# Forming the low parts of the filler weights by an accumulating DMA

## The chip, the cores and the metric

The kernel runs on one NeuronCore of a Trainium2 chip. A core has engines that work side by side, each through its own instructions in order: TensorE (PE in the profile, with its weight loads as PEld), VectorE (DVE), ScalarE (ACT), GpSimd (POOL) and SyncE (SP), which here issues most DMAs. The number that counts is the device time of one execution in microseconds. The kernel before takes 875.28 us (median of 3 runs, 873.97 to 875.67).

## The reference

One decoder block on 512 tokens of width 1024. After a modulated RMSNorm, one wide projection `w_in` feeds two token mixers, multi-head latent attention (MLA) and native sparse attention (NSA). Each mixer's output goes through its own output weights, and a sigmoid gate for each token and channel, also a product with `w_in`, weighs the two before they are added:

```
y_mla = mla_attention(...) @ w_o_mla
y_nsa = nsa_attention(...) @ w_o_nsa
merged = sigmoid(g_mla_merge) * y_mla + sigmoid(g_nsa_merge) * y_nsa
x = x + gt1 * (merged @ w_out)
x = x + gt2 * ((silu(h2 @ w_gate) * (h2 @ w_up)) @ w_down)
```

`g_mla_merge` and `g_nsa_merge` are the last 2048 columns of `h @ w_in`.

## The kernel before

**High and low parts.** The matmuls take operands of type fp32r, which holds fewer bits than float32. To keep the precision the kernel splits every operand into a high part (the value rounded to fp32r) and a low part (what the rounding took away, again as fp32r) and makes three products: high by high, high by low, low by high. For weights this is done by `wchunk`: it loads a chunk of up to 128 x 1024 floats into a tile `raw` (on SP's queue), ACT copies it into `whi` (`hi_of`, line 169), and another engine subtracts, `raw - whi`, into `wlo` (`lo_of`, line 172). The three tiles come from one pool, `wp`, with four buffers for each name, and all weights of the kernel share them. So at most four chunks are in preparation or use. A buffer of `raw` is free again when the low part has been formed, one of `whi` or `wlo` when the last matmul with it is done. In the first half of the kernel, SP loads the next chunk into a `raw` buffer as soon as it is free, whichever job asks for it; among them are strips of `ada_w` for the modulation vectors, which DVE multiplies and adds up into `macc`.

**Stages.** The projection runs first, then NSA (about 160 to 300 us), then MLA's latent products (300 to 350), MLA's attention (350 to 440), the output projections and the feed-forward part. Almost every instruction is recorded by the helper at line 152, so the profile gives L152 for all of them, and its groups are told apart by their tiles.

**Fillers.** The attention stages have chains of small steps through PE, DVE and ACT: scores, row minimum and mask (`mn`, on DVE), exponential (`s`, on ACT), row sums and scaling (`sm`), transposition on PE (`pt`), a split into `phi` (ACT) and `plo` (DVE), and the product with the values (`av`). To keep PE busy meanwhile, two side jobs are woven in:

- `gates()` makes the products for the merge gates. It has 16 jobs of one weight chunk (128 columns over the full depth of 1024) and 24 matmuls `gp` each. At a job's end ACT evacuates the sum through a tanh into `gs` and stores it to DRAM (`spill`).
- `y_nsa()` makes `nsa output @ w_o_nsa`: four chunks, each used for two sums `yn`, which DVE multiplies by the stored gate and POOL's queue stores.

Eleven of the gate jobs belong to the NSA stage (`D_GATES = 88` steps of 8 for each job), one lies between the stages, four and all of `y_nsa` belong to MLA's attention (`F_FILL = 64` steps). Both jobs get their chunks from `ahead`, which asks for a chunk one job before it is used, and with the arguments of `fill_lo`: which engine makes the low part, and into how many pieces the chunk is cut. Before the change that is POOL while the NSA stage is written down and DVE from line 1212 on (`fill_on[0] = dve`), with `FILL_CUT = 2`: the chunk's two halves are split one after the other. Twelve chunks get their low part on POOL, eight on DVE.

**Order of the work.** The kernel is written in a tile language. Each engine's order is not the order of the text: at the build a planner simulates a timeline with estimated durations (`schedule_with_timeline_sim=True`, line 1856) and lets each engine take what is ready, earlier text first. So a chunk asked for in the text one job ahead may be loaded and split as soon as buffers are free. `Paced` adds a few order constraints by hand: filler matmuls may not run ahead of the main work by more than a given count (`PACE_D`, `PACE_F`).

**POOL's other work** in these stages: scaling the selected probabilities in NSA and one row block of four in MLA (`s<-s,sm`), the low parts of the attention outputs (`onl`, `oml`), small square root steps, and the stores of `y_nsa`.

Of the kernel before, what the change touches and what calls it, by code (L numbers as in the profile page):

```python
# [15 lines left out]
ALU = mybir.AluOpType  # L16
# [17 lines left out]
FILL_CUT = 2  # L34
# [81 lines left out]
def hybrid_block(ctx, tc, a, out):  # L116
# [47 lines left out]
    pe, act, dve, pool, sp = (Paced(e) for e in (nc.tensor, nc.scalar, nc.vector, nc.gpsimd, nc.sync))  # L164

    def f32v(ap):
        return ap.bitcast(F32)

    def hi_of(dst, src, scale=1.0):
        act.activation(out=dst, in_=src, func=AF.Copy, scale=scale)  # L170

    def lo_of(dst, src, hi, eng=None):
        (eng or dve).tensor_tensor(out=dst, in0=src, in1=f32v(hi), op=ALU.subtract)
# [106 lines left out]
    def wload(src, parts, n):  # L280
        raw = wp.tile([P, 1024], F32, name="raw", tag="raw")
        rv = raw[:, : parts * n].rearrange("p (a n) -> p a n", a=parts)
        sp.dma_start(out=rv, in_=src)
        return raw

    def wchunk(src, parts, n, eng_lo=None, cut=1):
        raw = wload(src, parts, n)
        h = wp.tile([P, 1024], F32R, name="whi", tag="whi")
        l = wp.tile([P, 1024], F32R, name="wlo", tag="wlo")
        m = parts * n // cut  # L290
        for i in range(cut):
            c = slice(i * m, (i + 1) * m)
            hi_of(h[:, c], raw[:, c])
            lo_of(l[:, c], raw[:, c], h[:, c], eng_lo)
        return (h[:, : parts * n].rearrange("p (a n) -> p a n", a=parts),
                l[:, : parts * n].rearrange("p (a n) -> p a n", a=parts))

# [3 lines left out]
    fill_on = [pool]  # L301

    def fill_lo():
        return fill_on[0], FILL_CUT

    turn_at = [0]

# [65 lines left out]
    def gemm_tok(A, w, kt, c0, n, consume, tag="", eng_lo=None):  # L373
        ps = [mm.tile([P, S], F32, name=f"g{tag}{t}", tag="mm") for t in range(NT)]
        for k0 in range(0, kt, 2):
            parts = min(2, kt - k0)
            h, l = wchunk(rows(w, k0 * P, parts, c0, n), parts, n, eng_lo)
            for i in range(parts):
                k = k0 + i
                for t in range(NT):  # L380
                    ah, al = A(k, t)
                    pe.matmul(ps[t][:, :n], ah, h[:, i, :], start=(k == 0), stop=False)
                    pe.matmul(ps[t][:, :n], ah, l[:, i, :], start=False, stop=False)
                    pe.matmul(ps[t][:, :n], al, h[:, i, :], start=False, stop=(k == kt - 1))
            yield
        for t in range(NT):
            consume(t, ps[t][:, :n])
            yield

    def gemm_wide(A, w, kt, c0, na, nb, consume_a, consume_b, pair_first=False, eng_lo=None):  # L390
        pa = [mm.tile([P, S], F32, name=f"wa{t}", tag="mm") for t in range(NT)]
        pb = [sc.tile([P, 2, 256], F32, name=f"wb{j}", tag="sc") for j in range(2)]
        n = na + nb
        sa, sb = (slice(nb, n), slice(0, nb)) if pair_first else (slice(0, na), slice(na, n))
        ready = []

        def fetch(k):
            ready.append(wchunk(rows(w, k * P, 1, c0, n), 1, n, eng_lo))

        fetch(0)  # L400
        for k in range(kt):
            h, l = ready.pop()
            for t in range(NT):
                if t == FETCH_AT and k + 1 < kt:
                    fetch(k + 1)
                ah, al = A(k, t)
                for o, cs in ((pa[t][:, :na], sa), (pb[t // 2][:, t % 2, :nb], sb)):
                    first = k == 0 and (cs is sa or t % 2 == 0)
                    pe.matmul(o, ah, h[:, 0, cs], start=first, stop=False, skip_group_check=True)
                    pe.matmul(o, ah, l[:, 0, cs], start=False, stop=False, skip_group_check=True)  # L410
                    pe.matmul(o, al, h[:, 0, cs], start=False, stop=(k == kt - 1), skip_group_check=True)
            yield
        for t in range(NT):
            consume_a(t, pa[t][:, :na])
            if t % 2 == 1:
                consume_b(t - 1, pb[t // 2][:, 0, :nb])
                consume_b(t, pb[t // 2][:, 1, :nb])
            yield
# [435 lines left out]
    def compress_w1(i, nm):  # L854
        FS = cmp_state[i]
        ph = sc.tile([P, S], F32, name="ph", tag="sc") if i else mm.tile([P, S], F32, name="ph", tag="mm")
        cmp_state[i] = ph
        w1 = a[f"cmp_w1_{nm}"][0]
        for k0 in range(0, 16, 4):
            h, l = wchunk(rows(w1, k0 * P, 4, 0, 256), 4, 256)  # L860
            for j in range(4):
                pe.matmul(ph[:, :256], FS[:, k0 + j, :], h[:, j, :], start=(k0 + j == 0), stop=False)
                pe.matmul(ph[:, :256], FS[:, k0 + j, :], l[:, j, :], start=False, stop=(k0 + j == 15))
            yield
# [220 lines left out]
    def gates():  # L1085
        jobs = [(rows(w_in, 0, KD, SEG_C + c, P), KD, P) for c in range(0, 2 * D, P)]
        for i, (h, l) in enumerate(ahead(jobs, FILL_LEAD, fill_lo)):
            ps = mm.tile([P, S], F32, name="gp", tag="mm")
            for k in range(KD):
                turned_mm([ps], 0, hT[k], h[:, k, :], l[:, k, :], k == 0, k == KD - 1)  # L1090
                if k == KD - 1:
                    spill(ps, i)
                yield

    def y_nsa():
        jobs = [(rows(a["w_o_nsa"][0], 0, 4, c, 256), 4, 256) for c in range(0, D, 256)]
        for i, (h, l) in enumerate(ahead(jobs, FILL_LEAD, fill_lo)):
            for j in range(2):
                ps = mm.tile([P, S], F32, name="yn", tag="mm")
                at = 2 * i + j  # L1100
                gate = spill_src["pool"].tile([P, S], F32, name="gx", tag="gx", bufs=1)
                sp.dma_start(out=gate, in_=spilled[2 + at // 4][at % 4])
                for k in range(4):
                    turned_mm([ps], j * P, (on_h[k], on_l[k]), h[:, k, :], l[:, k, :], k == 0, k == 3)
                    if k == 3:
                        spill(ps, 16 + at, gate)
                    yield
# [752 lines left out]
```

## Time and profile before

| | |
|---|---|
| median of 3 runs | 875.28 us |
| profiled execution | 874.82 us |
| its span, first to last instruction | 873.0 us |
| PE busy | 841.4 us (96%) |
| DVE busy | 668.7 us (77%) |
| ACT busy | 457.2 us (52%) |
| POOL busy | 119.2 us (14%) |
| DMA, all queues | 115.54 MB, 132 GB/s |

All times of the trace are microseconds from the first instruction. A row of a group reads: line, engine, operation, output tile `<-` input tiles, shape, count, then busy time, mean duration in ns, and the idle time of that engine just before, with what ended it. "POOL waits for ACT whi" means that the last thing that POOL needed was ACT's instruction that writes `whi`. An engine's idle time matters only where PE, or the end of the kernel, waits for that engine. The granted clock (PEclk) is the share of full speed at which TensorE may run. The profiled execution's 874.82 us contain the span of 873.0 us and 1.8 us around it.

### The profile page before, as it was taken

To read this page: it belongs to the slowest core of one execution; us is meant where nothing else is said; L and a number is where in the kernel's file an instruction comes from. 1 tells how busy PE (TensorE), PEld (TensorE's weight loads), DVE (VectorE), ACT (ScalarE), POOL (GpSimd) and SP (SyncE) were. 2 spreads that over 40 slices of the span, in tenths; PEclk is the share of its full clock that TensorE was granted. 3 is DMA by queue.
4 is the path that set the end of the run, shared out by engine and by line. 5 is a ranking of instruction groups with operands and counts; after the bars stand their busy time and mean duration, and the time that the engine had idled before them with its cause. 6 is when DMAs were issued, how large, how long until landed. Compare 5 with 4: busy or idle time off the path is not lost.

```text
span 873.0 us, 13961 instructions
## 1 busy us (share of the span) xinstructions
PE 841.4 (96%) x5052; PEld 740.4 (85%) x5052; DVE 668.7 (77%) x1392; ACT 457.2 (52%) x962; POOL 119.2 (14%) x203
## 2 busy tenths in 40 slices
PE   8899799899999999899999999999999999999997
PEld 8789689777777789787788889898999889988996
DVE  5778896668888568688879877975887858965875
ACT  4643655678666567665634255551456326641550
POOL 0002516525342012212200000000000000000000
PEclk9999799999999999999999999999999999999999
DMA  9956646222201123325597753452233313343312
GB/s 309 326 166 189 197 143 170 74 72 74 72 13 61 43 92 98 120 97 180 172 321 253 256 166 118 128 152 90 73 98 121 121 51 113 104 125 92 98 49 97
DMA packets 95706, 115.54 MB, mean 132 GB/s; under 512 B 6565, under 2 KB 68885, under 8 KB 95637
## 3 DMA queue, kind: packets, MB, share of 16 engines
q1 hardware_dynamic: 92596, 108.32, 40.4%
q10 hardware_dynamic: 2400, 4.23, 1.3%
q0 software_dynamic: 640, 2.10, 0.6%
q8 instruction: 40, 0.66, 0.3%
q14 instruction: 30, 0.24, 0.1%
HBM read 106.24 MB, written 8.39 MB: 131 GB/s over the span
## 4 chain that ended last, share of the span: by engine, by line
PE 79%; DVE 8%; DMA 7%; ACT 3%; issue 2%; SPq 1%; ACTq 0%; DVEq 0%
PE d L152 14%; PE fx L152 12%; PE gp L152 9%; PE fy L152 9%; PE pt L152 4%; DMA strip<-in_ada_w_dram 4%; PE av L152 3%; PE ga L152 3%; PE gwo L152 3%; PE gym L152 3%; PE fg L152 3%; PE yn L152 3%; PE wo L152 3%; PE gq L152 2%; PE fu L152 2%
## 5 line engine op out<-in xcount | busy, mean ns | idle before, releaser
L152 ACT ACTIVATE whi<-raw 128x1024 fp32r<-128x1024 f32 (+4 forms) x161 | 141.6, 897 | 133.1 <-PE d L152 51.6
L152 DVE TENSOR_TENSOR wlo<-raw,whi 128x1024 fp32r<-128x1024 f32 (+4 forms) x138 | 149.4, 1090 | 61.3 <-ACT whi L152 60.8
L152 PE MATMUL d<-whi,mh 128*128 128x512 f32 (+1 forms) x180 | 69.9, 391 | 0.6 <-DVE tm L152 0.5
L152 PE MATMUL d<-wlo,mh 128*128 128x512 f32 (+1 forms) x180 | 70.2, 390 | 0.0
L152 PE MATMUL d<-whi,ml 128*128 128x512 f32 (+1 forms) x180 | 67.6, 389 | 0.0
L152 ACT ACTIVATE s<-s,mn 128x384 f32<-128x384 f32 (+2 forms) x96 | 52.5, 548 | 23.1 <-DVE mn L152 22.5
L152 DVE TENSOR_TENSOR plo<-pt,phi 128x512 fp32r<-128x512 f32 (+2 forms) x78 | 46.3, 602 | 19.1 <-ACT phi L152 18.7
L152 PE MATMUL gp<-hTh,whi 128*128 128x512 f32 x128 | 54.4, 425 | 0.0
L152 ACT ACTIVATE phi<-pt 128x512 fp32r<-128x512 f32 (+2 forms) x78 | 39.9, 525 | 27.5 <-PE pt L152 26.9
L152 PE MATMUL gp<-hTh,wlo 128*128 128x512 f32 x128 | 51.2, 400 | 0.0
L152 PE MATMUL gp<-hTl,whi 128*128 128x512 f32 x128 | 50.7, 396 | 0.0
L152 ACT ACTIVATE whi<-s 128x1024 fp32r<-128x1024 f32 (+1 forms) x36 | 30.2, 846 | 32.0 <-PE d L152 18.0
L152 PEld LDWEIGHTS d<-whi,mh 128*128 128x128 f32 x180 | 33.7, 188 | 8.9 <-DVE tm L152 1.2
L152 PE MATMUL fx<-h2h,whi 128*128 128x256 f32 x144 | 41.1, 286 | 0.0
L152 PE MATMUL fx<-h2l,whi 128*128 128x256 f32 x144 | 40.8, 283 | 0.0
L152 PE MATMUL fx<-h2h,wlo 128*128 128x256 f32 x144 | 40.8, 283 | 0.0
L152 PEld LDWEIGHTS d<-whi,ml 128*128 128x128 f32 x180 | 33.8, 188 | 7.7
L152 PEld LDWEIGHTS d<-wlo,mh 128*128 128x128 f32 x180 | 33.8, 188 | 7.4
L152 DVE TENSOR_TENSOR wlo<-s,whi 128x1024 fp32r<-128x1024 f32 (+1 forms) x36 | 33.7, 951 | 7.4 <-ACT whi L152 7.4
L152 PE MATMUL pt<-ident,s 128*128 128x128 f32 x232 | 37.4, 278 | 0.1
L152 POOL TENSOR_TENSOR wlo<-raw,whi 128x512 fp32r<-128x512 f32 x24 | 31.7, 1341 | 23.1 <-ACT whi L152 23.1
L152 PEld LDWEIGHTS pt<-ident,s 128*128 128x128 f32 x232 | 28.1, 142 | 7.6 <-issue 2.1
(432 smaller groups left out, 2666.2 us busy)
## 6 DMA issues: line engine op xcount, KB each, us to landing
raw<-in_ffn_w_gate_dram SPq DMA_DIRECT2D x22, 512.0 KB, 3.9
raw<-in_ffn_w_up_dram SPq DMA_DIRECT2D x22, 512.0 KB, 4.1
raw<-in_ffn_w_down_dram SPq DMA_DIRECT2D x22, 512.0 KB, 3.9
raw<-in_ada_w_dram SPq DMA_DIRECT2D x18, 512.0 KB, 5.0
araw<-in_ada_w_dram SPq DMA_DIRECT2D x32, 256.0 KB, 6.4
raw<-in_w_in_dram SPq DMA_DIRECT2D x16, 512.0 KB, 4.8
strip<-in_ada_w_dram SPq DMA_DIRECT2D x14, 512.0 KB, 5.2
raw<-in_w_in_dram SPq DMA_DIRECT2D x12, 352.0 KB, 3.2
```

The costliest lines, as they stand in the source:

```text
L152: out = call(*args, **kw)
```

## The change

The filler chunks, and only they, get their low part in another way. ACT writes the negated high part into `wlo` (the same rounding of the same values, with a scale of -1), and then a DMA on POOL's queue adds `raw` to what stands in `wlo`. The sum `raw - whi` is the same as before. The chunk is no longer cut in two, and `fill_lo` says so for all 20 filler chunks, whatever `fill_on` holds.

```
         for i in range(cut):
             c = slice(i * m, (i + 1) * m)
             hi_of(h[:, c], raw[:, c])
-            lo_of(l[:, c], raw[:, c], h[:, c], eng_lo)
+            if eng_lo == "dma":
+                hi_of(l[:, c], raw[:, c], -1.0)
+                pool.dma_start(out=l[:, c], in_=raw[:, c], accum_op=ALU.add)
+            else:
+                lo_of(l[:, c], raw[:, c], h[:, c], eng_lo)
...
     def fill_lo():
-        return fill_on[0], FILL_CUT
+        return "dma", 1
```

All other weights keep their subtraction on DVE. The buffer of `raw` is now in use until the DMA has landed.

## The prediction

> **What bounds the kernel now.** I read the page first, then busy time by stretch, then the waits of PE in the stretch that the edit touches, then the chain of waits.
>
> ```profile
> span 873.0 us, 13961 instructions
> ...
> PE 841.4 (96%) x5052; PEld 740.4 (85%) x5052; DVE 668.7 (77%) x1392; ACT 457.2 (52%) x962; POOL 119.2 (14%) x203
> ```
>
> PE is busy for 841.4 of 873.0 us, so 31.6 us of the span are not matmul time. The edit touches the 20 weight chunks of the two fillers (16 of the merge gates, 4 of the NSA output), which are prepared and used between 145 and 447 us. This is the busy time by stretch there (columns: us, then PE, weight loads, DVE, ACT, POOL, with instructions in brackets, then clock, DMA share, GB/s).
>
> ```profile
> 165.00:300.00 135.00, 130.77 (x654) 102.18 (x655) 104.59 (x312) 93.48 (x261) 46.00 (x62) 0.97 0.18 55
> 300.00:348.00 48.00, 46.99 (x258) 42.77 (x257) 33.71 (x96) 33.05 (x115) 10.01 (x38) 1.00 0.30 86
> 348.00:447.00 99.00, 94.19 (x513) 78.02 (x511) 77.69 (x190) 59.04 (x150) 19.00 (x32) 1.00 0.49 159
> sum 302.00, PE 290.82 PEld 240.37 DVE 224.16 ACT 196.19 POOL 87.60; mean PE 72.71 PEld 60.09 DVE 56.04 ACT 49.05 POOL 21.90
> ```
>
> The sum row covers 145 to 447 us: PE stands still for 302.0 - 290.8 = 11.2 us in it, DVE is busy for 74%, ACT for 65%, POOL for 29%. Those 11.2 us are the most that any relief of another engine can win, clock aside, since the edit leaves every matmul as it is. Who is last when PE waits:
>
> ```profile
> PE ps L152 <- DVE mn L152: 4.0, 6, 1.8
> PE av L152 <- ACT phi L152: 2.6, 5, 1.6
> PE pw L152 <- DVE mn L152: 2.1, 4, 0.6
> PE gk L152 <- ACT whi L152: 0.6, 1, 0.6
> PE pw L152 <- DVE sm L152: 0.6, 1, 0.6
> PE gk L152 <- DVE wlo L152: 0.4, 1, 0.4
> PE av L152 <- DVE plo L152: 0.2, 1, 0.2
> ```
>
> (total us, times, longest.) These are softmax statistics (mn, sm) and turned probabilities (phi, plo), apart from 1.0 us at gk, whose chunks the edit leaves alone. No wait of PE for the low part of an edited chunk is here: gp and yn are not in the list.
>
> **The change, part by part.** The rows that price it:
>
> ```profile
> L152 POOL TENSOR_TENSOR wlo<-raw,whi 128x512 fp32r<-128x512 f32 x24 | 31.7, 1341 | 23.1 <-ACT whi L152 23.1
> L1076 POOL DMA_DIRECT2D spill<-gs x8 | 4.8, 601 | 31.7 <-DVE gs L152 15.5 <-DVE mn L152 9.8 <-DVE sm L152 6.4
> L152 DVE TENSOR_TENSOR wlo<-raw,whi 128x512 fp32r<-128x512 f32 x16 | 10.4, 684 | 1.4 <-ACT whi L152 1.3
> L152 ACT ACTIVATE whi<-raw 128x1024 fp32r<-128x1024 f32 x88 | 93.4, 1062 | 113.0 <-PE d L152 51.6 <-PE fy L152 18.1 <-DMA raw<-in_w_out_dram 9.0
> ...
> spill<-gs POOLq DMA_DIRECT2D x8, 256.0 KB, 3.9
> raw<-in_w_in_dram SPq DMA_DIRECT2D x16, 512.0 KB, 4.8
> ```
>
> *Removed.* The 24 POOL and 16 DVE subtractions on half chunks: 31.7 us of POOL, 10.4 us of DVE. 24 + 16 halves are the 20 chunks.
>
> *Added on ACT.* One negated copy for each chunk, of the same size as a whole high part: 20 x 1.062 = 21.2 us. The high part itself is made in one piece where it was two; two halves in a row occupy 1.15 us (rows below) against 1.06, so 20 x 0.09 = 1.8 us go. Net +19.4 us: ACT between 145 and 447 us goes from 196.2 to 215.6 of 302 us, 65% to 71%.
>
> *Added on POOL.* 20 DMA issues. The eight plain ones on this queue take 0.60 us each, so about 12 us; POOL is still 31.7 - 12 = 20 us lighter. Each issue waits for ACT's negated copy where the subtraction waited for the high part, 1.06 us earlier. Behind it in POOL's queue stand the scaling of the selected probabilities, the low parts of the attention outputs and, later, the stores of gated rows. POOL is busy for 19.0 of 99 us in the last stretch and in nobody's row among the waits of PE, so I take 0.
>
> *Added on the DMA engines.* 20 transfers of 512 KB that also read their destination. No row shows an accumulating transfer. Near end: 3.9 us to landing for a plain 256 KB one from this queue. Far end: three streams of 512 KB (read source, read destination, write) instead of two of 256 KB, three times that, 11.7 us. I take 6, a little above the 4.8 us of a plain 512 KB load, and keep both ends. Nothing below 3.9 is likely, as the plain transfer is half the size.
>
> *How late a low part may be.* Low part and PE's use of it lie far apart (the first row: duration min/median/max in ns, first and last start; the others: start, us, what):
>
> ```profile
> L152 PE MATMUL gp<-hTh,wlo x9: 392/397/628, 159.5 to 175.8; 128*128 128x512 f32 x9
> ...
> 146.52 1.15 ACT L152 ACTIVATE whi<-raw 128x512 fp32r<-128x512 f32 x2 [3.55 <-PE ga L152]
> ...
> 158.38 1.15 ACT L152 ACTIVATE whi<-raw 128x512 fp32r<-128x512 f32 x2
> 159.44 0.37 ACT L152 ACTIVATE KH<-pk 128x256 fp32r<-128x256 f32 x1
> ...
> 172.54 1.15 ACT L152 ACTIVATE whi<-raw 128x512 fp32r<-128x512 f32 x2 [0.20 <-POOL s L152]
> ...
> 209.28 0.58 ACT L152 ACTIVATE gs<-gp 128x512 f32<-128x512 f32 x1
> ```
>
> Four buffers of each kind let ACT take up the fifth chunk at 172.5 us; the fourth job is evacuated (gs) at 209.3, and only then is the fifth chunk needed: 37 us. The new path from the start of the high part is 1.06 + 1.06 + 0.60 + 6 = 8.7 us, at the far end 14.4. So the accumulating transfer itself is covered by three jobs of matmuls. Without that cover each chunk would cost about 5.4 us (8.7 less the 0.6 + 2 x 1.34 = 3.3 us of now on POOL), 108 us in all. The first chunk has least room: taken up at 146.5, it would land at 155.2, at the far end 161, and its first job uses it at 159.5. So 0, with up to 2 us at the far end.
>
> *What lies on the path.* ACT and DVE, in order, serve the softmax loops whose ends PE waits for. PE waits for ACT 2.6 + 0.6 = 3.2 us. As an estimate, waits behind a queue grow with s/(1-s) for a busy share s: 0.65 gives 1.86, 0.71 gives 2.45, so +32%, **+1.0 us** (bounds 0 and, with all 20 copies in front of something that PE waits for, +21.2). DVE loses its 10.4 us nearly all in 300 to 447 us, where it is busy for 111.4 of 147: 76% becomes 69%, factor 0.70. Of ps's 4.0 us all but the longest 1.8 lies there, with the 0.4 at gk: 2.6 x 0.30 = **-0.8 us** (bounds 0 and -2.6). At the start of NSA, the copy for the chunk of 158.38 may push KH at 159.44 back, which the keys' scores need: 0 to +1.06, I take **+0.5**. Sum: **+0.7 us**.
>
> The profiled execution took 874.82 us (span 873.0 and 1.8 around it), 0.46 under the median 875.28. By the sum it would take 875.5, and the median becomes **876.0 us**. Under 0.2% (1.75 us) is about what this measurement can't tell from no change, so 873.5 to 877.0 counts as the same.
>
> **Rivals.** *ACT becomes the pace (slower).* High parts are taken up just when a job ends, directly in front of that job's evacuation and the next phi, and some are already in the chain:
>
> ```profile
> 283.80 0.62 ACT whi L152
> ...
> 359.62 0.61 ACT whi L152
> 360.23 0.48 ACT gs L152
> ...
> 379.65 0.64 ACT whi L152
> 380.31 1.29 DVE wlo L152 x2
> 381.63 3.83 DMA raw<-in_ada_w_dram
> 385.49 1.06 DVE macc L152
> ...
> 391.19 0.64 ACT whi L152
> ```
>
> If the copy stands there too, four times 1.06 and once more in front of KH: +5.3, **880.6 us**. It decides once the copy goes ahead of gs and phi in ACT's order and PE's filler behind the waiting av is used up. For it: ACT is the engine that gets the work, and the longest wait of av, 1.6 us, is just such a place (whi, gs, phi at 359.6). Against it: the build's planner places by simulated readiness and program order, and the copy's chunk stands late in program order.
>
> *Buffers come back late (slower).* Raw buffers are now held until the transfer lands. At 379.65 the high part starts, the buffer is free at 381.6, and an ada_w strip follows into it; its sum (macc) sits on DVE in front of the softmax. The new path frees the buffer 8.7 us after 379.65 instead of 2.0: macc 6.7 us later (4.6 at the near end of the landing). If DVE keeps its order, one such place costs PE up to 4.6 to 6.7 us: 880 to 882, I say **881**. Against: the planner orders DVE by its own simulated times and may put macc later. The Trainium skill, "SBUF — State Buffer", section "Who interferes with whom", speaks against this change: it says that GpSimd's descriptor generation is locked out while VectorE runs in a two-port mode. That would land the transfers still later; the 0.60 us per issue above, in a time when DVE is busy for three quarters, does not show it for plain transfers.
>
> *The start of NSA closes up (faster).* PE is thin there and its clock falls:
>
> ```profile
> 162.00:166.00 4.00, 1.87 (x13) 1.47 (x11) 1.58 (x8) 3.20 (x9) 1.61 (x5) 1.00 0.50 131
> 166.00:170.00 4.00, 3.37 (x20) 2.78 (x20) 3.15 (x20) 3.27 (x15) 0.00 (x0) 1.00 0.01 4
> 170.00:174.00 4.00, 3.48 (x17) 2.87 (x17) 3.24 (x18) 3.01 (x11) 2.33 (x5) 0.72 0.00 0
> 174.00:178.00 4.00, 4.00 (x11) 2.85 (x10) 1.76 (x5) 2.84 (x10) 1.77 (x2) 0.50 0.21 23
> 178.00:182.00 4.00, 4.00 (x20) 3.16 (x21) 3.23 (x13) 2.80 (x11) 0.52 (x2) 0.93 0.53 174
> ```
>
> After 2.1 + 0.6 us of standstill the granted clock is 0.72, 0.50, 0.93 in three slices of 4 us: 4 x (0.28 + 0.50 + 0.07) = 3.4 us lost. A new plan that fills 162 to 166 with gate matmuls keeps the clock up: **871.9 us** (875.28 - 3.4), and with DVE's 2.6 us of the later loops too, 869.3. The Trainium skill, "TensorE: Matmul & The Clock Gate", section "Part 1: The HAM clock gate (the "warmup" mystery)", ties the half clock to a free-running activity window of about 3.4 us; the trace agrees in that a thin stretch comes first. The same mechanism can work the other way, with a second dip.
>
> That the change does not do what it says I give nothing of its own: the new branch is taken for every filler chunk.
>
> **How the numbers follow.** Small effects that cancel, 876.0: 0.42 (0.39 of it within 0.2%, 0.03 above). ACT as the pace: 0.20. Late buffers: 0.15. A better start: 0.23. So faster 0.23, same 0.39, slower 0.38. The range, 871.0 to 882.5, takes in the likely size of each rival; outside are both slower rivals together and a start that closes up with all of DVE's waits gone. The likeliest case's own range is 873.5 to 878.
>
> **What would show it.** In the changed profile: no wlo subtraction on POOL, 16 fewer on DVE; 20 more activations of about 1.06 us; 20 accumulating issues on POOL near 0.6 us, landing in 4 to 12 us; PE's waits between 145 and 447 us near 11 us; none of gp or yn for wlo. I am wrong if av waits for phi by over 5 us (first rival), if DVE stands for macc's strips by over 4 us (second), if the clock stays at 1.00 through 170 to 182 us (third), or if gp or yn waits for a transfer, which would mean a landing of some 30 us.

## The result and the profile after

The changed kernel takes 886.54 us (median of 4 runs, 884.41 to 889.88); the kernel before, on the same chip, 874.62 us (872.75 to 875.67). The ratio is 1.0142, with a 95% interval of 1.0105 to 1.0179: slower by some 12 us, outside the range forecast. The profiled execution is the one of 884.41 us.

The head of the page after:

```profile
span 882.6 us, 13971 instructions
...
PE 842.8 (95%) x5052; PEld 741.8 (84%) x5052; DVE 659.4 (75%) x1376; ACT 473.2 (54%) x962; POOL 103.2 (12%) x199
```

The work went nearly as costed: PE has the same 5052 matmuls and the same busy time within 1.4 us, DVE 9.3 us less (forecast: 10.4), ACT 16.0 us more (19.4), POOL 16.0 us less (20). Only the span is longer, by 9.6 us. These rows price the new steps (the first two: busy us, mean ns, idle time in front; the third: KB and median us from issue to landing):

```profile
L152 ACT ACTIVATE wlo<-raw 128x1024 fp32r<-128x1024 f32 x20 | 21.1, 1053 | 5.5 <-PE ga L152 5.5
L296 POOL DMA_DIRECT2D wlo<-raw x20 | 17.8, 888 | 94.4 <-ACT wlo L152 75.2 <-PE ps L152 9.8 <-ACT onh L152 9.5
wlo<-raw POOLq DMA_DIRECT2D x20, 512.0 KB, 4.6
```

Busy time by stretch, in the columns of the prediction's table:

```profile
165.00:300.00 135.00, 130.75 (x669) 102.93 (x670) 99.77 (x308) 100.33 (x264) 32.84 (x57) 1.00 0.38 93
300.00:348.00 48.00, 47.00 (x259) 42.85 (x258) 31.96 (x93) 34.58 (x116) 11.37 (x40) 1.00 0.35 97
348.00:447.00 99.00, 86.41 (x456) 71.03 (x455) 70.60 (x170) 60.09 (x140) 20.17 (x35) 0.97 0.60 168
sum 302.00, PE 282.25 PEld 233.42 DVE 210.94 ACT 209.65 POOL 69.56; mean PE 70.56 PEld 58.36 DVE 52.74 ACT 52.41 POOL 17.39
```

NSA and the latent products are as before. In the last row, MLA's attention, PE is busy for 86.4 us where it was 94.2: 7.8 us more of standstill, and the mean clock is 0.97 instead of 1.00, which over 99 us is another 3 us. In these 99 us PE gets 57 matmuls fewer done than before. No engine is near its limit there: DVE is busy for 71%, ACT for 61%, POOL for 20%. So it is not an engine's pace but waits at certain places. The waits of PE between 145 and 447 us (total us, times, longest):

```profile
PE av L152 <- ACT phi L152: 8.6, 6, 2.4
PE ps L152 <- DVE mn L152: 4.9, 4, 1.9
PE av L152 <- DVE plo L152: 2.7, 4, 1.2
PE pw L152 <- DVE mn L152: 2.1, 4, 0.6
PE gk L152 <- ACT whi L152: 0.6, 1, 0.6
PE gk L152 <- DVE wlo L152: 0.4, 1, 0.4
```

`av` waits for `phi` for 8.6 us instead of 2.6, `ps` for 4.9 instead of 4.0, `av` for `plo` for 2.7 instead of 0.2. Neither `gp` nor `yn` waits for a transfer. What holds `phi` up is in the chain of waits (start, us, what), at two of the job ends:

```profile
381.21 0.58 ACT gs L152
381.79 0.36 ACT wlo L152
382.14 0.49 issue
382.63 0.97 ACT s L152 x4
...
383.63 0.60 ACT of L152
384.23 0.01 issue
384.24 0.61 ACT phi L152
384.85 0.04 issue
384.89 0.51 PE av L152
...
395.81 0.44 ACT gs L152
396.25 0.04 issue
396.28 1.06 ACT wlo L152
397.34 0.35 issue
397.69 4.56 DMA wlo<-raw
...
402.31 3.65 DMA raw<-in_ada_w_dram
...
405.98 0.75 DVE macc L152
406.73 0.66 DVE kl L152
```

At 381.8 us the negated copy (`ACT wlo`) stands between the gate's evacuation and the softmax, and the `phi` for which `av` waits comes behind it. At 396.3 us the second mechanism follows on the first: copy, transfer (4.56 us), and only when it has landed can SP load the next strip of `ada_w` into that `raw` buffer (402.31); `macc` on DVE waits for the strip, and `kl` of the next head comes behind `macc`. The first two strips of this stage are issued at 387.7 and 402.3 us, before the change at 381.6 and 393.2. SP's own waits show that it stands seven times until such a transfer has landed, for weight chunks as well as for strips; where a load is early enough, that costs nothing. First the kernel before, 347 to 439 us, then the changed one, 344 to 447 us:

```profile
SPq L152 <- DVE wlo L152: 35.2, 6, 12.1
```

```profile
SPq L152 <- DMA wlo<-raw: 60.5, 7, 16.0
```

In MLA's attention, where the clock was 1.00 before, it falls twice, where PE has just stood still (slices of 4 us, the clock is the third number from the end):

```profile
384.00:388.00 4.00, 3.11 (x11) 2.54 (x12) 3.35 (x9) 3.58 (x9) 1.10 (x2) 0.73 0.69 131
388.00:392.00 4.00, 4.00 (x21) 3.26 (x19) 2.26 (x4) 0.69 (x1) 0.87 (x1) 0.84 0.43 131
...
396.00:400.00 4.00, 2.28 (x13) 1.68 (x12) 2.56 (x8) 3.95 (x10) 0.89 (x1) 0.94 0.43 115
400.00:404.00 4.00, 4.00 (x15) 3.29 (x14) 2.78 (x7) 1.80 (x5) 0.70 (x1) 0.64 0.57 94
```

That is 4 x (0.27 + 0.16 + 0.06 + 0.36) = 3.4 us. Not every standstill does it: behind the longest, 2.4 us at 357 to 360 us, the clock stays at 1.00. The clock where it fell before, at the start of NSA, stays up:

```profile
162.00:166.00 4.00, 2.12 (x13) 1.67 (x12) 1.98 (x12) 3.54 (x13) 0.00 (x0) 1.00 0.91 205
166.00:170.00 4.00, 2.87 (x21) 2.35 (x20) 3.53 (x22) 3.02 (x15) 0.26 (x1) 1.00 0.30 90
170.00:174.00 4.00, 4.00 (x23) 3.13 (x23) 3.02 (x15) 3.53 (x9) 1.31 (x4) 1.00 0.03 8
174.00:178.00 4.00, 4.00 (x22) 3.27 (x22) 2.85 (x12) 4.00 (x16) 1.02 (x2) 1.00 0.80 184
178.00:182.00 4.00, 4.00 (x26) 3.37 (x25) 3.03 (x12) 2.37 (x10) 1.39 (x4) 1.00 0.56 140
```

For comparing kernels I take the stretch from the first `gk` matmul (start of MLA's latent products) to the first `gym` matmul (end of its attention); these rows give their first and last start. Before:

```profile
L152 PE MATMUL gk<-whi,cTh x16: 388/394/499, 306.1 to 332.7; 128*128 128x512 f32 x16
L152 PE MATMUL gym<-omh,whi x32: 389/389/799, 438.3 to 462.9; 128*128 128x512 f32 x32
```

After:

```profile
L152 PE MATMUL gk<-whi,cTh x16: 392/394/501, 302.7 to 329.3; 128*128 128x512 f32 x16
L152 PE MATMUL gym<-omh,whi x32: 389/389/791, 446.3 to 470.9; 128*128 128x512 f32 x32
```

That is 132.2 us before and 143.6 us after: 11.4 us lost, while `gk` starts 3.4 us earlier. PE's busy time in it is 126.4 us before and 130.0 after, so 7.8 of the 11.4 us are standstill and 3.6 are the same matmuls taking longer. "MLA's stretch" below is this difference, always of one profiled execution; in two executions of the same work it differed by 0.8 to 3.1 us (e9, e10 and e12 below).

### The profile page after: what moved, and what is told of

The parts are those of the page before. It is cut to its first block, busy times and chain, and to the rows that moved or that the text cites. A ratio compares the mean times of both kernels' runs of the same rounds, so it can differ in the third digit from the quotient of the medians.

```text
span 882.6 us, 13971 instructions
## 1 busy us (share of the span) xinstructions
PE 842.8 (95%) x5052; PEld 741.8 (84%) x5052; DVE 659.4 (75%) x1376; ACT 473.2 (54%) x962; POOL 103.2 (12%) x199
## 4 chain that ended last, share of the span: by engine, by line
PE 76%; DVE 9%; DMA 6%; ACT 4%; issue 3%; SPq 1%; ACTq 0%; DVEq 0%
PE d L152 14%; PE fx L152 12%; PE gp L152 9%; PE fy L152 9%; PE pt L152 4%; PE av L152 3%; PE ga L152 3%; PE fg L152 3%; PE gwo L152 3%; PE gym L152 3%; PE wo L152 2%; PE fu L152 2%; DMA strip<-in_ada_w_dram 2%; PE gq L152 2%; DVE s L152 2%
## 5 line engine op out<-in xcount | busy, mean ns | idle before, releaser
L152 ACT ACTIVATE whi<-raw 128x1024 fp32r<-128x1024 f32 (+3 forms) x141 | 140.1, 996 | 131.4 <-PE d L152 51.6
L152 DVE TENSOR_TENSOR wlo<-raw,whi 128x1024 fp32r<-128x1024 f32 (+3 forms) x122 | 138.0, 1135 | 60.5 <-ACT whi L152 60.0
L152 ACT ACTIVATE s<-s,mn 128x384 f32<-128x384 f32 (+3 forms) x96 | 52.3, 547 | 11.7 <-DVE mn L152 11.4
L152 PE MATMUL ga<-wlo,hTh 128*128 128x352 f32 x96 | 31.1, 325 | 0.4 <-DVE rq_m_kc L152 0.4
```

The source lines that it names most:

```text
L152: out = call(*args, **kw)
```

## The experiments

Theories, named as in the expectations: (A) the negated copy on ACT stands in front of `phi`; (B) the transfer gives the `raw` buffer back late, and loads on SP and `macc` on DVE come late; and, formed on the way, (C) the chunk in one piece instead of two costs; (D) the planner's new order of the instructions costs, whatever the cause; (W) against (D), the added work itself. A ratio is to the kernel before on the same chip and at the same time, with its 95% interval.

### One stage, or one part, at a time

*e1*, the change for NSA's 12 chunks only:

```
-        return "dma", 1
+        return ("dma", 1) if fill_on[0] is pool else (dve, FILL_CUT)
```

> Only the 12 chunks of the NSA stage take the accumulating DMA; the 8 of MLA's attention keep the two half subtractions on DVE. Theory A (the copy on ACT stands in front of phi at the job ends of MLA's attention) and theory B (the transfer holds raw and low part too long there) expect the same here: MLA's attention as before, no av wait over 1.6 us behind phi, and the gain at the start of NSA kept if the new plan is what closed the clock dip: 870 to 873 us. If the loss were spread over both stages: 878 to 882 us.

Measured: 874.56 us, 0.9972 [0.9942, 1.0002]; MLA's stretch 133.4 us.

*e2*, the change for MLA's 8 chunks only:

```
-        return "dma", 1
+        return (pool, FILL_CUT) if fill_on[0] is pool else ("dma", 1)
```

> The reverse: POOL subtracts halves in NSA, the 8 chunks of MLA's attention take copy and accumulating DMA. Both theories: the loss is here, 11 to 13 us over before, 885 to 888 us, and the clock dip at 170 to 182 us is back. If the two stages act on each other through the plan, anything between 875 and 885.

Measured: 883.59 us, 1.0081 [1.0049, 1.0113]; MLA's stretch 137.7 us. The loss is in MLA, since e1 shows none. But e2 has the same work in MLA as the change and loses 0.81%, not 1.42%, and its stretch grows by 5.5 us, not 11.4: e1 and e2 together do not make up the change.

*e3*, the copy without the transfer:

```
                 hi_of(l[:, c], raw[:, c], -1.0)
-                pool.dma_start(out=l[:, c], in_=raw[:, c], accum_op=ALU.add)
+                lo_of(l[:, c], raw[:, c], h[:, c], fill_on[0])
```

> The negated copy on ACT as in the change, but then the whole subtraction on POOL or DVE over it in place of the DMA: the ACT work of the change without any transfer, and DVE and POOL keep theirs. Theory A: av waits for phi as in the change (7 us or more in MLA's attention), 884 to 890 us. Theory B: nothing is held for a transfer, so 874 to 878 us.

Measured: 881.78 us, 1.0063 [1.0029, 1.0096]; MLA's stretch 135.6 us.

*e4*, the transfer without the copy on ACT (GpSimd negates the high part):

```
-                hi_of(l[:, c], raw[:, c], -1.0)
+                pool.tensor_scalar(out=l[:, c], in0=f32v(h[:, c]), scalar1=-1.0, scalar2=None, op0=ALU.mult)
                 pool.dma_start(out=l[:, c], in_=raw[:, c], accum_op=ALU.add)
```

> The accumulating DMA as in the change, but the negation of the high part on POOL, from the high part: ACT has 20 instructions fewer, the transfer starts about 0.4 us later. Theory A: av's waits for phi go back to 2 to 3 us, and with DVE relieved the time is 868 to 875 us. Theory B: the transfer is as late as in the change, so 882 to 888 us.

Measured: 883.38 us, 1.0072 [1.0044, 1.0101]; MLA's stretch 139.0 us. Each half of the change alone costs about half of the loss: 0.63% and 0.72%, together 1.35% where the change has 1.42%. In MLA's stretch they add 3.4 and 6.8 us to the 132.2 of before, together 10.2 of 11.4 (e3 also lost at the start of NSA, where its clock fell for longer). So neither (A) nor (B) alone. e4 is not quite the transfer by itself, though: GpSimd takes 2.80 us for a negation where ACT took 1.05, so `raw` is held longer than in the change. And `av` waits for `phi` for 4.7 us of MLA's stretch in e4, without any copy on ACT (before: 2.2, e3: 3.8), so that wait is not a mark of the copy alone. All three slow kernels also had something else in common: chunks in one piece, a first wait of `av` for `phi` of 2.4 us instead of 1.6, and another order on PE.

### The cut, the place of the negation, another engine

*e5* (from e1): MLA's chunks by DVE, in one piece.

```
+        return ("dma", 1) if fill_on[0] is pool else (dve, 1)
```

> NSA's 12 chunks by the accumulating DMA as in e1; MLA's 8 chunks by a subtraction on VectorE as in e1, but high part and subtraction each in one piece instead of two halves. No DMA and no extra copy in MLA. Theories: (A) ACT's negated copy stands in front of phi, (B) the transfer frees the raw buffer late: neither is here, so the time stays at e1's 874.6 (873 to 876). (C) the chunk in one piece is what costs, since all slow kernels so far share it and share a first av-for-phi wait of 2.4 us instead of 1.6: most of e2's loss without any transfer, 879 to 884. (D) the planner lays out another order of filler and softmax as soon as durations change, and that order is worse whatever the cause: 877 to 884, with DVE's waits for ps at 5 us or more instead of 2.8.

Measured: 876.20 us, 0.9978 [0.9955, 1.0000]; MLA's stretch 132.8 us. (C) falls.

*e6*: the change in two halves.

```
-        return "dma", 1
+        return "dma", 2
```

> The change with its chunks in two halves: 40 negated half copies and 40 accumulating DMAs of 256 KB instead of 20 of 512 KB. (A) ACT does slightly more (20 x 0.1 us): 886 to 889. (B) the first half lands earlier, the second about 1 us later than now: 884 to 888. (C) with the halves back the loss of MLA goes: 874 to 878. (D) a third order: anything from 876 to 888; PE's order tells.

Measured: 888.50 us, 1.0100 [1.0071, 1.0129]; MLA's stretch 142.2 us. Halves do not help: (C) falls again. The interval meets that of the change, so whether it is better or worse than that stays open.

*e7*: DVE negates the high part, then the transfer.

```
-                hi_of(l[:, c], raw[:, c], -1.0)
+                dve.tensor_scalar(out=l[:, c], in0=f32v(h[:, c]), scalar1=-1.0, scalar2=None, op0=ALU.mult)
```

> The change with the negated copy made by VectorE from the high part (20 whole chunks), then the accumulating DMA: ACT has none of the extra copies, DVE about what it had before. (A) the extra ACT copies were the cost: 875 to 879. (B) or (C): as e4, where GpSimd negated, 882 to 886. (D) 877 to 886 by the order that comes out.

Measured: 884.47 us, 1.0094 [1.0060, 1.0128]; MLA's stretch 139.4 us. With ACT free of the copies the loss stays, as in e4. In it `av` waits for `phi` for 1.7 us only, and DVE stands for `macc`'s strips for 7.0 us (before: 1.3): without (A), (B) is what is left of the two. DVE also has the negations themselves in its queue, 0.69 us each.

*e8* (from e1): MLA's low parts by half subtractions on GpSimd; no transfer, no copy, DVE relieved of them.

```
+        return ("dma", 1) if fill_on[0] is pool else (pool, FILL_CUT)
```

> NSA by the accumulating DMA as in e1; MLA's low parts by half subtractions on GpSimd instead of VectorE: DVE loses 10.4 us in MLA as in the change, with no transfer, no copy, no whole piece. PE's order in MLA stays nearly that of e1. (A), (B), (C) and (D) all say no loss: 872 to 875.5, the lower end if DVE's relief (my -0.8 us, at most -2.6) is real; above 877 would mean that taking the work off DVE is itself harmful.

Measured: 879.87 us, 1.0038 [1.0011, 1.0065]; MLA's stretch 137.1 us. No theory expected a loss against e1. In this profile `pt` waits once for 3.2 us for DVE's scaling, and DVE waits for `macc`'s strips for 3.3 us. The relief of DVE, which the prediction put at -0.8 us, does not come; the interval is above that of e1. The relief is not bare here: a half takes 1.30 us on GpSimd, 0.68 on VectorE, so `raw` is held somewhat longer, and GpSimd has these halves in front of its own work. That spoke for (D): edits which have little in common all lose a few us here.

### Late buffers

*e9*: the change, with an edit meant to give the strips of `ada_w` two buffers of their own during MLA's attention (a pool `stp`, closed behind it).

```
+    strip_src.update(pool=st_st.enter_context(tc.tile_pool(name="stp", bufs=1, ...)), bufs=2)
     with tc.tile_pool(name="mat", bufs=2, side="right", reuse_waits="tile") as mat:
...
+    strip_src.clear()
     pe.gate = mla_last
+    st_st.close()
```

> The change, with the strips of the modulation weights (ada, summed into macc on VectorE) in two buffers of their own during MLA's attention, so that they no longer wait for a raw buffer that an accumulating DMA still reads. (B) late buffers are the cost: most of MLA's 11 us come back, 875 to 879, and VectorE's wait for the strips falls below 1 us. (A) ACT's copy in front of phi: no gain from buffers, 884 to 888. (D) the order of the plan: it is laid out anew here too, 876 to 888.

Measured: 885.07 us, 1.0123 [1.0082, 1.0165]; MLA's stretch 146.7 us. The edit did not take hold. No strip is written down in this part of the text (`F_MODS = 0`); the strips that run during MLA's attention are written behind it, where the new buffers are closed again, and the planner pulls them forward. In the trace they still go into `raw` (the first two at 391.3 and 405.9 us), and every engine has the same instructions in the same order as in the change. So e9 is the change measured once more, and it says nothing about (B). Its ratio agrees with that of the change.

*e10*: the same strip buffers in the kernel before.

> The kernel before with the same two strip buffers: the control. All theories: 872 to 876.5; the strips cost VectorE 1.3 us before, which is the most that the buffers can give by themselves. Above 878 would mean that any new plan of this stage is worse than the one of before (D).

Measured: 874.63 us, 1.0015 [0.9988, 1.0043]; MLA's stretch 133.7 us. For the same reason this is the kernel before once more, in the same order on every engine; the ratio of 1.00 shows how well two measurements of it agree.

*e11* (from e1): each of MLA's chunks also read by a plain DMA from GpSimd into a scratch that nobody uses.

```
+        if cut == 2 and eng_lo is dve:
+            junk = dr.tile([P, 1024], F32, name="junk")
+            pool.dma_start(out=junk, in_=raw)
```

> e1 (NSA by the accumulating DMA, MLA by half subtractions on VectorE) plus, for each of MLA's 8 chunks, a plain DMA from GpSimd that reads the raw buffer and writes it to a scratch in DRAM that nobody uses: no copy on ACT, no low part that waits for a transfer, only the raw buffer held some 5 us longer. (B) loses as e2 did: 879 to 884. (A): as e1, 873 to 876. (D): 877 to 884, without a longer wait of VectorE for the strips.

Measured: 878.62 us, 1.0059 [1.0033, 1.0086]; MLA's stretch 135.1 us. This did not test what it was meant to. The plain DMA needs only `raw`, which is loaded far ahead: the last one is issued at 363.1 us, while the last high part is begun at 396.2 us. No buffer was held late (DVE waits 0.7 us for the strips). What it does show is that 8 more DMAs on GpSimd's queue are not free: the interval lies above e1's, with PE's order in MLA the same but for 6 places (by the tiles named in the two traces). That is where (D) had put the time, without a longer wait for the strips.

*e12*: e1 with the strip buffers.

> e1 with the two strip buffers: the likely best version. NSA's start keeps its clock (-2.5 us against before), VectorE's wait for strips (0.8 us in e1) goes. (A), (B): 872 to 875, e1 or a little better. (D): 872 to 880.

Measured: 874.62 us, 0.9996 [0.9972, 1.0020]; MLA's stretch 132.6 us. This is e1 once more, in the same order on every engine. No version here is shown to beat the kernel before.

### The order against the work

In these, an engine is held to the order that it has in the other kernel. `seen` lists an engine's instructions in the order of the text, without those that split filler chunks; `ORDERS` is the order that the planner gave them in the other kernel. The list of PE has the same 4,994 matmuls for the two kernels; 587 stand in other places, 214 of them from `gk` on. In the traces of e13 to e18 the engines that are held do run in the order asked for.

```
+            Paced.free or self.seen.append(ins); self.keep_order(ins)
...
+            for i, j in zip(order[:-1], order[1:]):
+                e.follow(e.seen[int(j)], e.seen[int(i)])
```

*e13*, the change, PE in the order of before:

> The changed kernel with PE's 4,994 matmuls held in the order that they have in the kernel before (587 places differ); the other engines are laid out around that. (D) the order is the cause and PE's order is what matters: 874 to 878. (D) but with DVE's or ACT's order as what matters: 880 to 887. (W) the added work itself (copies, transfers) is the cause, whatever the order: 883 to 889.

Measured: 888.94 us, 1.0148 [1.0105, 1.0191].

*e14*, the change, PE, DVE and ACT in the order of before:

> The changed kernel with PE, VectorE and ScalarE all held in the order of before; only the fillers' high parts, negated copies and DMA issues are placed freely. (D) 873 to 877. (W) 883 to 889, with PE waiting for phi behind the copies as in the changed kernel.

Measured: 896.80 us, 1.0235 [1.0202, 1.0269].

*e15*, the kernel before, PE in the order of the change:

> The kernel before, its subtractions unchanged, with PE's matmuls in the order of the changed kernel. (D) with PE's order as the cause: 881 to 887, MLA's attention near 102 us instead of 91. (W): 872 to 876.

Measured: 878.87 us, 1.0055 [1.0021, 1.0090].

*e16*, the kernel before, all three in the order of the change:

> The kernel before, its subtractions unchanged, with PE, VectorE and ScalarE in the order of the changed kernel; only the fillers' high parts and subtractions are placed freely. (D): 882 to 888, as the change itself, with no accumulating transfer and no negated copy in it. (W): 872 to 876.

Measured: 881.51 us, 1.0072 [1.0042, 1.0102].

e13 lies where (W) had put it, e14 above both ranges, e15 and e16 between the two. MLA's stretch in us, as a table (e1 and e12 have before's order on PE there too):

| | order of before | order of the change |
|---|---|---|
| work of before | 132.2, 133.7 (before, e10), 133.4, 132.6 (e1, e12) | 136.6 (e15, PE), 135.7 (e16, all) |
| work of the change | 141.1 (e13, PE), 148.2 (e14, all) | 143.6, 146.7 (the change, e9) |

Read down a column for the work, along a row for the order. The work costs 7 to 9 us in before's order on PE, 14 to 16 with all three engines held, 7 to 11 in the order of the change. The order alone costs 2 to 4 us of the stretch; in the medians of the whole kernel it is 0.55% and 0.72%, where the change costs 1.42%. So (D) is true for a part of the loss, up to half of it, and false as the cause: before's order does not bring the time back (1.0148), and with all three engines held it gets worse (1.0235). The planner's order seems to soften the added work, at a price. What that work does when nothing may move out of its way shows in e14, 311 to 451 us, in the waits of PE, then of DVE, then of SP's queue:

```profile
PE av L152 <- ACT phi L152: 8.3, 4, 4.1
PE ps L152 <- DVE mn L152: 4.9, 6, 1.8
```

```profile
DVE macc L152 <- DMA raw<-in_ada_w_dram: 9.8, 2, 4.9
```

```profile
SPq L152 <- DMA wlo<-raw: 63.6, 7, 16.0
```

Both mechanisms stand there: two strips come 4.9 us late each, just about one landing.

### The two parts in the order of before

*e17*: e3 (copy, no transfer), all three engines in the order of before.

> e3 (the negated copy on ACT for all 20 chunks, then the low part by a whole subtraction over it on GpSimd or VectorE; no DMA) with PE, VectorE and ScalarE in the order of before. (A) the copy in front of phi is the cost: 888 to 896, nearly e14's 1.0235 as a ratio. (B) the held buffer is the cost: 876 to 880, with VectorE's wait for the strips below 3 us. Both: 881 to 886.

Measured: 885.32 us, 1.0097 [1.0066, 1.0129]; MLA's stretch 141.8 us. The waits of PE and of DVE, 309 to 449 us:

```profile
PE av L152 <- ACT phi L152: 5.0, 5, 2.4
PE ps L152 <- DVE mn L152: 3.9, 5, 1.9
```

```profile
DVE macc L152 <- DMA raw<-in_ada_w_dram: 2.2, 2, 1.2
```

The copy without the transfer costs 0.97%, 8.5 us. `av` waits for `phi` for longer; the strips are nearly on time. The stretch of this execution is 9.6 us longer than before: 4.5 of standstill, and 5.1 of matmuls that took longer at a granted clock of 0.96. From e17 to e14 nothing changes but the subtraction, which becomes a transfer: 1.0097 to 1.0235, 1.4% or 12 us more, with the intervals far apart, and the mark is now DVE's wait for strips, 2.2 to 9.8 us. The time of e17 lies where "both" had put it.

*e18*: the kernel before, all three in its own order, with e11's plain DMA behind all 20 chunks.

> The kernel before with its own subtractions and its own order on PE, VectorE and ScalarE, and after each of the 20 chunks a plain DMA from GpSimd that reads the raw buffer into a scratch in DRAM (landing 4.5 us in e11, like the accumulating one's 4.6): only the buffer is held. (B): 884 to 892, SP waiting for that DMA for over 40 us in the last 100 us of the stretch and VectorE for the strips near e14's 9.8 us. (A): 874 to 878. Both: 879 to 884.

Measured: 885.95 us, 1.0101 [1.0048, 1.0153]; MLA's stretch 137.9 us. The time lies in (B)'s range, but none of (B)'s marks is there: as in e11 the plain DMA reads `raw` early (the last one is issued at 368.3 us, the last high part is begun at 404.6 us), SP waits for it for 1.7 us, and the strips cost DVE 1.0 us. So it is no evidence for (B). The profiled execution is 13.8 us longer than that of before, and 8.1 of them are lost before `gk`, where the clock is 0.50 in the five slices of 4 us from 166 to 186 us; 5.7 are lost in MLA's stretch. One place there is a wait of PE that neither the kernel before nor the change has (340 to 450 us):

```profile
PE pt L152 <- POOL s L152: 3.0, 1, 3.0
```

In front of this scaling of a softmax block, GpSimd's queue has DMA issues that wait until their chunk is loaded; two of them had stood for 11.0 and 2.6 us.

## Why the prediction was wrong

**What held.** The prices of the added steps: 20 copies of 1.05 us on ACT (21.1 us, forecast 21.2); a landing of 4.6 us, at most 7.7 (forecast 6, between 3.9 and 11.7); POOL's issue is dearer, 0.89 instead of 0.60 us, but nobody on PE waits for POOL. The cover of 37 us for a low part held: no filler matmul waits for a transfer.

**The step that failed** is the one under "What lies on the path". It spread ACT's added 19.4 us evenly over a queue, let waits grow by s/(1-s), and got +1.0 us. But the copies are not spread. Four gate jobs end in MLA's attention, and at each of them ACT now does the high part, the evacuation and the negated copy, and only then the softmax that PE waits for. The `av` behind these four wait for `phi` for 2.4, 1.4, 1.7 and 1.7 us; before, two of them waited at all, for 1.6 and 0.2. From 145 to 447 us this wait grew by 6.0 us (2.6 to 8.6), not by 32%. Not all of it is the copy: with the work of before in the order of the change, `av` waits for `phi` for 3.8 us (e15) and 4.1 us (e16) of MLA's stretch, in the change for 7.5, before for 2.2.

The sum also left the clock out. In the changed kernel's profile it falls at the last two of these four waits, and 3.6 of the 11.4 us of MLA's stretch are matmuls that took longer. The prediction says that "the same mechanism can work the other way, with a second dip", and gave that no price.

For DVE, -0.8 us was forecast for less work, but the waits for `mn` and `plo` grew by 0.9 and 2.5 us. Why is not shown. DVE's own wait for the strips grew only from 1.3 to 2.7 us. e8, which relieves DVE without copy and transfer in MLA, is slower than e1.

**The rivals.** The first slower one named the right place: four job ends, with the copy in front of `phi`, and its mark came (8.6 us, over 5). What spoke against it, that the copy's chunk "stands late in program order", did not hold. Of the second one, the late strip is in the chain at 402.3 us, but its mark is not clear: DVE stands for strips for 2.7 us, not over 4, though for 4.7 in e9, the same work once more. It is more than 4 us in e7 (7.0) and e14 (9.8) too, but also in e15 (4.3), which has no transfer. What shows that the transfer costs is e14 against e17. I took the two for alternatives, 0.20 and 0.15, and left "both slower rivals together" outside the range; e17 and e14 show that copy and transfer each cost, one on top of the other. That the two prices, +5.3 and about +5.7 us, add up to 11.0, close to the 11.9 us between the medians, is luck in part: in the order of before, copy and transfer cost 8.5 and 12 us, and in the order of the change some of the loss is the order's.

**The start of NSA** kept its clock in the profile, and `gk` starts 3.4 us earlier, just the size given. But the mechanism was another one: the gate matmuls did not fill 162 to 170 us, where PE stood still for 3.0 us, before for 2.8. And it is not an effect of the change that the runs can show. e12 is e1 once more, with the order of the change on PE up to `gk`, and its clock fell:

```profile
166.00:170.00 4.00, 3.81 (x13) 3.29 (x14) 2.20 (x14) 2.37 (x11) 0.00 (x0) 0.57 0.51 132
170.00:174.00 4.00, 2.94 (x19) 2.43 (x18) 3.50 (x20) 2.44 (x10) 1.42 (x4) 0.91 0.02 4
174.00:178.00 4.00, 4.00 (x13) 2.88 (x12) 1.95 (x10) 3.74 (x10) 0.71 (x2) 0.50 0.03 13
178.00:182.00 4.00, 4.00 (x19) 3.15 (x18) 1.10 (x6) 2.52 (x9) 0.32 (x1) 0.74 0.83 183
```

There `gk` starts at 307.9 us, 5.6 us later than in e1. In e10, the kernel before once more, the dip at this place is half as deep (1.7 us instead of 3.4). So a price that was read off one execution's dip belonged to the execution. What e1 leaves for the change in NSA is 0.28%, with no change inside its interval.

**What stays open.** Through what the transfer costs: strips that come late, weight loads that come late, or GpSimd's dearer issue. Buffers of their own for the strips were not tried, since e9's edit did not take hold, and e11 and e18 never held a buffer late. Nor was a queue of its own for the strips tried. That order matters by some us is shown (e2, with the same work in MLA as the change, has a stretch of 137.7 us), but not what makes one order better.

## What to carry to other kernels

An engine's share of the time says little about work that is put in at one fixed point of a cycle: ask what stands behind it at that point, and price that. When a cheap operation is replaced by a slow asynchronous one that keeps its source buffer, the consumer may have all the slack in the world; look also at who wants the buffer next. Two mishaps that can both happen are no alternatives: give that case a chance. And before an experiment is read, see in its trace that the edit took hold: e9 looked like a test of the buffers, and its strips still went into `raw`.

## What the runs showed of the hardware

An accumulating DMA of 512 KB from SBUF to SBUF takes 0.89 us to issue on GpSimd, against 0.60 us for a plain one of 256 KB in the kernel before and for the plain ones of 512 KB in e18, and lands after 4.6 us. The plain ones of 512 KB, from SBUF to DRAM, landed in 4.5 us in e11 and 4.0 us in e18 (medians). Whether the dearer issue comes from the accumulation, the fp32r destination or the way from SBUF to SBUF, no run separates.

The granted clock can fall in one execution and stay up in another of the same instructions in the same order on every engine: in e1 it is 1.00 from 162 to 186 us, in e12 it falls to 0.50. In the six kernels with the same work in NSA and the same order on PE up to `gk` (the change, e1, e5, e8, e9, e12), `gk` starts between 302.3 and 307.9 us. The Trainium skill, "TensorE: Matmul & The Clock Gate", section "Part 1: The HAM clock gate (the "warmup" mystery)", says that the window over which activity is watched runs freely, and that the point of change depends on where in it the first matmul lands. That it matters in the same way where in it a thin stretch falls is inferred; e1 and e12 agree with that, and neither shows the window itself.
